# Retention's up projection by seven-product units, with mixer operands that carry the token scale

## The chip, the cores and the metric

The kernel runs on one core of one Trainium2 chip, which executes the whole program once. The metric is the device time of that execution in microseconds (us); lower is better. A kernel's time is the median of several executions.

## The reference

One decoder layer on 1024 tokens of 1024 features, in float32. Cut to what the change touches:

```python
h = rmsnorm(x, ln_mix)                 # x * rsqrt(mean(x^2)+eps) * ln_mix
z = h @ w_in                           # q | k | v | g | pu | gate_logits
ret = retention_chunkwise(rotary(q) * dk**-0.5, rotary(k), v)      # 4 heads, 8 chunks of 128
ret_n = group_norm_per_head(ret) * gn_gain
y_ret  = (silu(g) * ret_n) @ w_ret_up                              # 1024 x 1024
y_pool = (multiscale_pool(pu, windows 2/4/8/16) @ pool_w * pool_scale) @ w_pool_up
gates = sigmoid(gate_logits + b_gate)
x = x + (gates[:, :D] * y_ret + gates[:, D:] * y_pool) @ w_o
x = x + square(relu(rmsnorm(x, ln_mlp) @ w_up)) @ w_down
out = rmsnorm(x, ln_final)
```

The token scale is the `rsqrt(...)` of the first line, one number for each token.

## The kernel before

**Numbers as pairs.** Every float32 operand of a large product is carried as a pair of rounded halves, the value and its remainder (`split_pair`: one copy on ScalarE, line 134, one subtraction on VectorE, line 135). A product of two pairs is three matmuls (value by value, value by remainder, remainder by value; `PASSES`). Activations lie feature-major: 128 features on the partitions, 512 tokens (half of the sequence) in a matmul.

**Stages, in the order of TensorE's queue.** Rotary, values and retention for four heads; `pool_input(g)`, four projections to the pool channels (`ps_pu`), beside the last head; twelve *mixer units* (`ps_Xmx`, `ps_Ymx`, `ps_Zmx`, `ps_Vmx`); retention's up projection (`ps_yr`, line 630) with `pool(g)` beside it; the pool's up projection (`ps_yp`); the output projection (`ps_o`); sixteen units of the feed-forward's up projection (`ps_Xup` and so on); its down projection (`ps_dn`).

**A seven-product unit** (`seven`) computes a 256 x 1024 piece of a product as two by two blocks, by seven block products in place of eight. X, Y, Z and V are four banks of PSUM. A unit has an opening product in each bank and a closing one in X, Z and V, of 4 x 3 = 12 matmuls each, 84 in all. It needs seven stationary operands, sums of weight blocks that VectorE adds (line 192) and that are split into pairs in tag "a", and seven moving operands, each of four feature tiles, which all units of a stage share. These are combinations of the token halves of the low and high features: B11, B21 and B22 are blocks as they are, T1 to T4 are sums and differences. After a closing the function `done` finishes a quarter of the result. The first of a stage (`late`) interleaves its openings over feature tiles.

**The mixer units.** Units 0 to 3 make the swish gate g, units 4 to 11 the two branch gates. Their B operands are the tiles of `hT` (x times ln_mix, in tag "h"); `mixed_blocks` makes the T operands from another load of x in tag "r". The token scale `R1` is not in them: `done` multiplies every quarter of the result by R1 on VectorE (line 559, 566). Swish units then apply a sigmoid and multiply by the normalized retention and by gn_gain; all others apply a sigmoid, with the bias. Results go to DRAM (`ret_dram`, `sg_dram`).

**Retention's up projection** loads `ret_dram` back (`load_ret` in unit 11), splits it into 16 pairs `retT`, and makes 8 feature tiles x 2 token halves, each by 8 x 3 matmuls (384 in all), from weights loaded and split by `load_piece`. The result times the gate stays in SBUF (`m`). `pool(g)` runs after every second of these feature tiles: VectorE adds shifted copies of `u`, and six matmuls (`ps_pw`) follow for each g.

**What sets the order.** All of it is written as one program with tiles from tagged pools: tags "h" and "r" have 16 buffers of 512 KB each, "a" has 9, of which R1 holds one in the mixers; tag "raw" has two. A scheduler with a model of the engines' times then sets, before the run, each engine's own fixed sequence. On the chip every engine works through its sequence strictly in that order and waits where a tile is not ready or a buffer not free. Loads are issued by SyncE (SP), stores and some loads by GpSimd (POOL); these queues also stop at an issue that waits.

Of the kernel before, what the change touches and what calls it, by code (L numbers as in the profile page):

```python
# [30 lines left out]
NLAST = 4  # L31
EPS = 1e-6
# [6 lines left out]
def block_kernel(ctx: ExitStack, tc: tile.TileContext, a: dict, out: bass.AP):  # L39
# [12 lines left out]
    idle = apool.tile([P, HALF], mybir.dt.bfloat16, tag="a", name="idle", bufs=9)  # L52
# [123 lines left out]


    B11, B21, B22, T1, T2, T3, T4 = range(7)

    def seven(name, src, moving, done, late=False, after=None):  # L180
# [9 lines left out]
        def stationary(x, src, *adds):  # L190
            for dst, u, v in adds:
                nc.vector.tensor_tensor(dst, u, v, ALU.add)  # L192
            ws[x] = pair_tile("a", f"w{x}_{name}")
            split_pair(ws[x], src)
# [52 lines left out]
    def token_blocks(lo, hi):  # L247
        return lo[:, :HALF], lo[:, HALF:], hi[:, :HALF], hi[:, HALF:]
# [225 lines left out]

    q, k, v = [None] * NH, [None] * NH, [None] * NH
# [3 lines left out]
    for h in range(NH):  # L479
# [52 lines left out]
    ret_dram = dram_tile("ret_dram", (KT // 2, P, 2, S))  # L532
    sg_dram = dram_tile("sg_dram", (2 * KT, P, S))

    def mixer_unit(i, late=False, after=None):
# [4 lines left out]
        if swish:  # L540
            for m, f in enumerate(tiles):
                nc.gpsimd.dma_start(o[m], retn_dram[f])
        left = [2, 2]

        def done(m, half, ps, add=None):
            sl = slice(half * HALF, (half + 1) * HALF)
            dst, f = o[m][:, sl], tiles[m]
            sign = -1.0 if m else 1.0
            if swish:
                t = rpool.tile([P, 2, HALF], F32, tag="raw", name=f"sw{f}_{half}")  # L550
                z, sig = t[:, 0, :], t[:, 1, :]
# [6 lines left out]
            if swish:  # L558
                nc.vector.scalar_tensor_tensor(z, y, sign, R1[:, sl], ALU.mult, ALU.mult)
                nc.scalar.activation(sig, z, AF.Sigmoid)  # L560
                nc.vector.scalar_tensor_tensor(
                    dst, dst, vec[:, V_GNG + f : V_GNG + f + 1], sig, ALU.mult, ALU.mult
                )
                nc.vector.tensor_tensor(dst, dst, z, ALU.mult)
            else:
                nc.vector.tensor_tensor(z, y, R1[:, sl], ALU.mult)
# [9 lines left out]
    retT = []  # L576

    def load_ret():
        for p2 in range(KT // 2):
            r2 = w_tile(f"ret{p2}", F32).rearrange("p (i t) -> p i t", i=2)  # L580
            nc.sync.dma_start(r2, ret_dram[p2])
            for i in range(2):
                retT.append([])
                for half in range(2):
                    dst = pair_tile("h" if p2 < 2 else "r", f"retT{2 * p2 + i}_{half}")
                    split_pair(dst, r2[:, i, half * HALF : (half + 1) * HALF])
                    retT[-1].append(dst)

    for i in range(12):
        mixer_unit(i, late=i == 0, after=load_ret if i == 11 else None)  # L590


    pw_raw, pw = a_tile("r", "pw_raw", shape=(P, HALF)), pair_tile("r", "pw")
    nc.sync.dma_start(pw_raw, a["pool_w"])
    split_pair(pw, pw_raw)
    ypT = []

    def pool(g):
        win = WINDOWS[g]
        u = a_tile("r", f"uf{g}")  # L600
        nc.sync.dma_start(u, u_dram[g])
        cur = u
        step = 1
        while step < win:
            nx = a_tile("r", f"s{g}_{step}")
            nc.vector.tensor_copy(nx[:, :step], cur[:, :step])
            nc.vector.tensor_tensor(nx[:, step:], cur[:, step:], cur[:, : S - step], ALU.add)
            cur = nx
# [472 lines left out]
```

## Time and profile before

| | us |
|---|---|
| three runs | 1373.17, 1372.91, 1370.94 (median 1372.91) |
| the profiled execution's own time | 1370.83 |
| its span, from the first to the last instruction | 1369.0 |
| TensorE (PE) busy | 1353.6 (99%) |
| VectorE (DVE) busy | 987.9 (72%) |
| ScalarE (ACT) busy | 565.1 (41%) |
| mean granted clock of TensorE | 0.997 |

Busy times are from one profiled execution; the profile models the end of a matmul, so a busy PE says that matmuls are in flight. "PEclk" is the clock that was granted to TensorE, as a share of full speed. In a list of groups each row is a source line with its engine, operation and tiles (out<-in), then the count, the summed busy time and the mean duration, then the idle time of that engine just before these instructions and what ended it. The stages on the trace's clock: mixers from 285 to 515 us, `ps_yr` to 612, `ps_yp` to 654, up from 740 to 1060, down to the end.

### The profile page before, as it was taken

Reading aid. Unit: us, or ns where it says so; the run is one execution under the profiler, and the core shown is the slowest. Engines: PE = TensorE matmul, PEld = TensorE weight load, DVE = VectorE, ACT = ScalarE, POOL = GpSimd, SP = SyncE. Lnnn points to the kernel's source line nnn. Section 1 sums busy time; section 2 is a strip of 40 time slices with the busy share of each in tenths; the row PEclk is TensorE's granted clock in tenths of the full one; section 3 lists DMA queues with packets and bytes.
Section 4 is the critical chain, followed back from the end, with each engine's and each line's share of the span. In section 5 each row is a group of like instructions: output and inputs, shape, how many; then the busy total and the mean of one; then the engine's idle time right before and its main releaser. Section 6 shows DMA issues by size and latency. Waiting matters only on the chain. (4 is left out here: it accounts for less than half of the span.)

```text
span 1369.0 us, 17491 instructions
## 1 busy us (share of the span) xinstructions
PE 1353.6 (99%) x6572; PEld 1138.6 (83%) x6572; DVE 987.9 (72%) x1631; ACT 565.1 (41%) x960; POOL 86.1 (6%) x151
## 2 busy tenths in 40 slices
PE   9999999999999999999999999999999999999997
PEld 6998999878888888888887888888888888888886
DVE  5766565789966768628657878777787977689665
ACT  6234425463334344113445433333333544444372
POOL 0000001111000000000001011101111000000000
PEclk9999999999999999999999999999999999999999
DMA  9122021354342367124422344433437989778423
GB/s 360 50 62 77 17 92 63 124 215 158 121 172 85 112 238 261 62 77 170 154 77 77 116 169 169 151 126 147 169 139 292 407 330 351 261 266 307 159 70 123
DMA packets 65444, 225.07 MB, mean 164 GB/s; under 512 B 7376, under 2 KB 9424, under 8 KB 61264
## 3 DMA queue, kind: packets, MB, share of 16 engines
q1 hardware_dynamic: 47152, 158.66, 32.7%
q0 software_dynamic: 17920, 65.02, 12.5%
q8 instruction: 51, 0.84, 0.3%
q10 hardware_dynamic: 288, 0.29, 0.1%
q14 instruction: 33, 0.27, 0.1%
HBM read 167.31 MB, written 56.62 MB: 164 GB/s over the span
## 5 line engine op out<-in xcount | busy, mean ns | idle before, releaser
L121 PE MATMUL ps_v<-w_v_hi,hT 128*128 128x256 f32 x512 | 96.0, 284 | 0.0
L199 PE MATMUL ps_Xup<-mv,w_up 128*128 128x512 f32 x384 | 93.0, 390 | 1.7 <-DVE w_up L135 1.7
L199 PE MATMUL ps_Zup<-mv,w_up 128*128 128x512 f32 x384 | 92.5, 389 | 0.8 <-ACT w_up L134 0.8
L853 PE MATMUL ps_dnX<-db,da 128*128 128x512 f32 x384 | 93.1, 389 | 0.1
L134 ACT ACTIVATE w_up<-raw_up 128x512 fp32r<-128x512 f32 x96 | 58.3, 627 | 84.4 <-DVE raw_up L192 46.3
L199 PE MATMUL ps_Vup<-mv,w_up 128*128 128x512 f32 x384 | 92.6, 389 | 0.0
L121 PE MATMUL ps_yr<-retT,w_ret 128*128 128x512 f32 x384 | 88.5, 389 | 0.5 <-ACT w_ret L94 0.5
L121 PE MATMUL ps_o<-mixT,w_o 128*128 128x512 f32 x384 | 87.5, 389 | 0.0
L199 PEld LDWEIGHTS ps_Xup<-mv,w_up 128*128 128x128 f32 x384 | 71.9, 188 | 16.9 <-DVE w_up L135 2.1
L121 PEld LDWEIGHTS ps_yr<-retT,w_ret 128*128 128x128 f32 x384 | 72.0, 188 | 15.8 <-ACT w_ret L94 0.9
L199 PEld LDWEIGHTS ps_Zup<-mv,w_up 128*128 128x128 f32 x384 | 72.0, 188 | 15.7 <-ACT w_up L134 0.8
L853 PEld LDWEIGHTS ps_dnX<-db,da 128*128 128x128 f32 x384 | 72.0, 188 | 15.5 <-DVE db L135 0.5
L199 PEld LDWEIGHTS ps_Vup<-mv,w_up 128*128 128x128 f32 x384 | 72.0, 188 | 15.1 <-ACT w_up L134 0.2
L121 PEld LDWEIGHTS ps_o<-mixT,w_o 128*128 128x128 f32 x384 | 72.0, 188 | 15.0
L135 DVE TENSOR_TENSOR w_up<-raw_up,w_up 128x512 fp32r<-128x512 f32 x96 | 64.2, 685 | 26.4 <-ACT w_up L134 26.1
L121 PEld LDWEIGHTS ps_v<-w_v_hi,hT 128*128 128x128 f32 x512 | 80.8, 192 | 0.0
L134 ACT ACTIVATE w_mx<-raw_mx 128x512 fp32r<-128x512 f32 x72 | 43.6, 626 | 86.0 <-DVE raw_mx L192 44.0
L121 PE MATMUL ps_v<-w_v_lo,hT 128*128 128x256 f32 x256 | 72.6, 284 | 0.0
L199 PE MATMUL ps_Xmx<-hT,w_mx 128*128 128x512 f32 x288 | 72.0, 396 | 0.3 <-ACT w_mx L134 0.3
L199 PE MATMUL ps_Vmx<-hx,w_mx 128*128 128x512 f32 x288 | 69.5, 389 | 0.0
L728 ACT ACTIVATE act<-act 128x512 f32<-128x512 f32 x64 | 40.3, 629 | 65.6 <-DVE act L727 62.2
L199 PEld LDWEIGHTS ps_Xmx<-hT,w_mx 128*128 128x128 f32 x288 | 55.1, 192 | 12.5 <-ACT w_mx L134 0.6
(249 smaller groups left out, 2819.9 us busy)
## 6 DMA issues: line engine op xcount, KB each, us to landing
act_dram<-act POOLq DMA_DIRECT2D x48, 512.0 KB, 4.7
ad<-act_dram SPq DMA_DIRECT2D x48, 512.0 KB, 6.6
raw_up<-in_w_up_dram SPq DMA_DIRECT2D x16, 1024.0 KB, 5.0
raw_mx<-in_w_mix_dram SPq DMA_DIRECT2D x12, 1024.0 KB, 6.2
sg_dram<-mx POOLq DMA_DIRECT2D x16, 512.0 KB, 4.7
wa_lo<-in_w_down_dram SPq DMA_DIRECT2D x16, 512.0 KB, 9.0
wb_hi<-in_w_down_dram SPq DMA_DIRECT2D x16, 512.0 KB, 7.5
wc_lo<-in_w_down_dram SPq DMA_DIRECT2D x16, 512.0 KB, 4.3
```

The costliest lines, as they stand in the source:

```text
L121: nc.tensor.matmul(ps, stationary(k, sa), moving(k, sb), start=i == 0, stop=i == n - 1)
L134: nc.scalar.activation(dst[:, 0, :], src, AF.Copy)
L135: nc.vector.tensor_tensor(dst[:, 1, :], src, dst[:, 0, :].bitcast(F32), ALU.subtract)
L199: nc.tensor.matmul(ps, ws[x][:, sa, k * P : (k + 1) * P], moving[x][k][:, sb, :], start=start and k == 0 and n == 0, stop=k == 3 and n == ...
L728: nc.scalar.activation(dst, dst, AF.Square)
L853: nc.tensor.matmul(banks[i][:, c0 : c0 + n], w[:, sa, i * P : (i + 1) * P], x[:, sb, c0 : c0 + n], start=start and j == 0 and m == 0, stop ...
```

## The change

1. **The up projection of retention** becomes four seven-product units (`ret_unit`), 4 x 84 = 336 matmuls. The weights are laid out for it ahead of the run (`_units`). Results are multiplied by the gate, stored to `m_dram`, and loaded again beside the gate of the pool's branch in the `ps_yp` stage (`merge_parts`).
2. **All seven mixer operands** are built from x times ln_mix times R1 (one `scalar_tensor_tensor` for each of eight feature tiles), during retention (`BUILD` says after which head), as 28 pairs that go to `hx_dram` (28 x 512 KB) and are loaded into 16 "r" and 12 "h" tiles ahead of the mixers. `done` no longer multiplies by R1; gn_gain carries the sign (`gng`).
3. **Retention's moving operands** (`ret_blocks(k)`) are built the same way beside units 4, 6, 8 and 9, go to `rx_dram` and are loaded after unit 11's X bank is closed (`load_rx`).
4. **`pool(g)`** moves from the `ps_yr` stage to units 1, 3, 5 and 7 (`BESIDE`); its results go to `yp_dram` and are loaded in the last of the ret units.
5. **Buffers:** tag "a" has 5 in place of 9, a new tag "e" has 4. The mixers' stationary operands lie in "a", so five buffers (R1 is no longer held) where there were eight; the up projection of the feed-forward takes "a" and "e" in turn.

```diff
-    BUFS = {"h": 16, "r": 16, "a": 9}
+    BUFS = {"h": 16, "r": 16, "a": 5, "e": 4}
+BUILD = ((0,), (1,), (2, 3), ())
+BESIDE = {1: ("pool", 0), 3: ("pool", 1), 4: ("ret", 0), 5: ("pool", 2),
+          6: ("ret", 1), 7: ("pool", 3), 8: ("ret", 2), 9: ("ret", 3)}
+    def mixed_blocks(k):
+        blocks = []
+        for f in (k, k + 4):
+            xf = a_tile("e", f"xf{f}")
+            nc.vector.tensor_copy(xf[:, :1], R1[:, S - 1 :])
+            nc.gpsimd.dma_start(xf, a["xT"][f * P : (f + 1) * P, :])
+            nc.vector.scalar_tensor_tensor(
+                xf, xf, vec[:, V_LNM + f : V_LNM + f + 1], R1, ALU.mult, ALU.mult)
+            blocks.append(xf)
+        for x, src in moving_blocks(*blocks):      # 7 blocks, 4 of them by a sum or difference
+            t = pair_tile("e", f"hs{x}_{k}")
+            split_pair(t, src)
+            store_pair(hx_dram[4 * ORDER.index(x) + k], t)
 # mixer_unit, done():
             if swish:
-                nc.vector.scalar_tensor_tensor(z, y, sign, R1[:, sl], ALU.mult, ALU.mult)
-                nc.scalar.activation(sig, z, AF.Sigmoid)
+                nc.scalar.activation(sig, y, AF.Sigmoid, scale=sign)
                 nc.vector.scalar_tensor_tensor(
-                    dst, dst, vec[:, V_GNG + f : V_GNG + f + 1], sig, ALU.mult, ALU.mult
+                    dst, dst, gng[:, m, f : f + 1], sig, ALU.mult, ALU.mult
                 )
-                nc.vector.tensor_tensor(dst, dst, z, ALU.mult)
+                nc.vector.tensor_tensor(dst, dst, y, ALU.mult)
             else:
-                nc.vector.tensor_tensor(z, y, R1[:, sl], ALU.mult)
+    for i, x in enumerate(ORDER):                  # (B11, T2, T1, T3, B21, B22, T4)
+        for k in range(4):
+            hx[x][k] = pair_tile("rrrrhhh"[i], f"hx{x}_{k}")
+            load_pair(hx[x][k], hx_dram[4 * i + k])
+    def ret_blocks(k):                             # loads ret_dram[k], [k + 4] into tag "raw"
+        for x, src in moving_blocks(*blocks):
+            t = pair_tile("e", f"rs{x}_{k}")
+            split_pair(t, src)
+            store_pair(rx_dram[4 * ORDER.index(x) + k], t)
+    def load_rx():
+                rx[x][k] = pair_tile("errrhhh"[i], f"rx{x}_{k}")
+                load_pair(rx[x][k], rx_dram[4 * i + k])
-    for f in range(KT):
-        w = load_piece(a["w_ret"][f], f"w_ret{f}")
...
-            feature_major(ps, w, retT, half)
-            nc.vector.tensor_tensor(m[:, sl], m[:, sl], ps, ALU.mult)
+    def ret_unit(i, after=None):
+        def done(m, half, ps, add=None):
+            dst, y = o[m][:, half * HALF : (half + 1) * HALF], ps
+            if add is not None:
+                y = rpool.tile([P, HALF], F32, tag="raw", name=f"yr{tiles[m]}_{half}")
+                nc.vector.tensor_tensor(y, add, ps, ALU.add)
+            nc.vector.scalar_tensor_tensor(dst, y, -1.0 if m else 1.0, dst, ALU.mult, ALU.mult)
+            left[m] -= 1
+            if not left[m]:
+                nc.gpsimd.dma_start(m_dram[tiles[m]], o[m])
+        seven(f"ret{i}", a["w_ret"][i], rx, done, late=i == 0, after=after)
+    def merge_parts(f):                            # ps_yp stage: the gate's tile and m, from DRAM
+        nc.sync.dma_start(parts[f][:, 0, :], sg_dram[KT + f])
+        nc.sync.dma_start(parts[f][:, 1, :], m_dram[f])
```

The order of the engines' sequences changes with it. Three places follow.

TensorE where two mixer units meet. Before, units 3 and 4 (banks 3291 and 3292 are X and Y of unit 3, 3145 is Z and 3146 V of unit 2):

```order
1244 L199 MATMUL ps_Xmx_3291<-hT_0_163,w_mx_3295 128x512 x3
1245 L199 MATMUL ps_Xmx_3291<-hT_0_166,w_mx_3295 128x512 x3
1246 L199 MATMUL ps_Xmx_3291<-hT_0_169,w_mx_3295 128x512 x3
1247 L199 MATMUL ps_Xmx_3291<-hT_0_172,w_mx_3295 128x512 x3
1248 L199 MATMUL ps_Ymx_3292<-hx_0_2625,w_mx_3314 128x512 x3
1249 L199 MATMUL ps_Ymx_3292<-hx_1_2704,w_mx_3314 128x512
1250 L199 MATMUL ps_Zmx_3145<-hT_1_204,w_mx_3240 128x512 x3
```

After, units 4 and 5 (3804 and 3805 are X and Y of unit 5, 3637 is Y of unit 4; `ps_pw` belongs to `pool(1)`):

```order
1306 L213 MATMUL ps_Xmx_3804<-hx_3_2898,w_mx_3808 128x512 x3
1307 L392 MATMUL ps_pw_0_3610<-pooled_0_3607,pw_3602 128x512 x3
1308 L213 MATMUL ps_Xmx_3804<-hx_0_2924,w_mx_3843 128x512 x3
1309 L213 MATMUL ps_Xmx_3804<-hx_1_2926,w_mx_3843 128x512 x3
1310 L213 MATMUL ps_Xmx_3804<-hx_2_2928,w_mx_3843 128x512 x3
1311 L213 MATMUL ps_Xmx_3804<-hx_3_2930,w_mx_3843 128x512 x3
1312 L392 MATMUL ps_pw_1_3621<-pooled_1_3618,pw_3602 128x512
1313 L213 MATMUL ps_Ymx_3637<-hx_0_2900,w_mx_3659 128x512 x3
```

Before, a unit's Y follows its own X opening. Now the Y of unit 4 comes only behind unit 5's X opening and X closing, with its weights (3659) held in a buffer of "a" until then.

VectorE at the same place. Before, where unit 4's results are finished (`mx_0`, `mx_4`; 3704 and 3709 belong to the weights of unit 6):

```order
469 L556 TENSOR_TENSOR mx_0_3432<-tmp_mx_3436,ps_Zmx_3439 128x512
470 L192 TENSOR_TENSOR tmp_mx_3704<-raw_mx_3702 128x512
471 L566 TENSOR_TENSOR mx_0_3432<-mx_0_3432,R_130 128x512
472 L135 TENSOR_TENSOR w_mx_3709<-raw_mx_3702,w_mx_3709 128x512
473 L192 TENSOR_TENSOR raw_mx_3702<-raw_mx_3702 128x512
474 L556 TENSOR_TENSOR mx_4_3433<-tmp_mx_3436,ps_Vmx_3440 128x512
```

After (`raw_u` is the load of `pool(1)`, `win` its sums; 3743 is a weight of unit 4, 3808 to 3843 of unit 5):

```order
482 L559 COPY win_0_3594<-raw_u_3592 128x1
483 L560 TENSOR_TENSOR win_0_3594<-raw_u_3592 128x1023
484 L140 TENSOR_TENSOR w_mx_3743<-raw_mx_3633,w_mx_3743 128x512
485 L559 COPY win_1_3595<-win_0_3594 128x2
486 L560 TENSOR_TENSOR win_1_3595<-win_0_3594 128x1022
487 L140 TENSOR_TENSOR w_mx_3808<-raw_mx_3801,w_mx_3808 128x512
488 L140 TENSOR_TENSOR pw_3602<-pw_raw_3603,pw_3602 128x128
489 L563 TENSOR_TENSOR win_1_3595<-win_1_3595,corr 128x16
490 L206 TENSOR_TENSOR raw_mx_3801<-raw_mx_3801 128x512
491 L564 SCALAR_TENSOR_TENSOR win_1_3595<-win_1_3595,raw_u_3592 128x1024
492 L140 TENSOR_TENSOR w_mx_3827<-raw_mx_3801,w_mx_3827 128x512
```

The multiplications by R1 are gone, and the pool's rows stand between the weight splits, behind the load of `raw_u`.

SyncE's loads at the end of the mixers. Before:

```order
56 L182 DMA raw_mx_4372<-in_w_mix_dram 128x2048
57 L581 DMA ret_4431<-ret_dram 128x2048
58 L581 DMA ret_4445<-ret_dram 128x2048
59 L626 DMA m_4570<-sg_dram 128x1024
60 L626 DMA m_4629<-sg_dram 128x1024
```

After (`r` is the last load of `ret_blocks`, `raw_ret` the weights of a ret unit, `rx` the operands):

```order
98 L647 DMA r_4611<-ret_dram 128x1024
99 L189 DMA rx_0_4847<-rx_dram 128x1024
100 L189 DMA rx_1_4849<-rx_dram 128x1024
101 L189 DMA rx_2_4851<-rx_dram 128x1024
102 L196 DMA raw_ret_4970<-in_w_ret_dram 128x2048
103 L189 DMA rx_0_4839<-rx_dram 128x1024
```

Four loads of 1 MB and then the gates become 28 loads of operands, each into a tile that an earlier product must free, with the weights of a ret unit queued among them.

More of the change, by code (lines that the diff above doesn't have):

```diff
@@ L524, in block_kernel, with pool @@
-    pool_input(0)
-    for g in range(1, 4):
+    def pool(g):
+        win = WINDOWS[g]
+        cur = u = load_raw(u_dram[g], f"u{g}")
+        two = [a_tile("e", f"win{g}_{i}") for i in range(min(2, win // 2))]
+        step = 1
+        while step < win:
+            nx = two[(step.bit_length() - 1) % 2]
+            nc.vector.tensor_copy(nx[:, :step], cur[:, :step])
+            nc.vector.tensor_tensor(nx[:, step:], cur[:, step:], cur[:, : S - step], ALU.add)
+            cur = nx
+            step *= 2
+        nc.vector.tensor_tensor(cur[:, :16], cur[:, :16], corr[:, g, :], ALU.mult)
+        nc.vector.scalar_tensor_tensor(cur, cur, 1.0 / win, u, ALU.mult, ALU.subtract)
+        pw = consts.tile([P, 2, P], F32R, tag="mask", name=f"pw{g}")
+        pw_raw = rpool.tile([P, P], F32, tag="raw", name=f"pw_raw{g}")
+        nc.sync.dma_start(pw_raw, a["pool_w"][:, g * P : (g + 1) * P])
+        split_pair(pw, pw_raw)
+        for half in range(2):
+            pooled = pair_tile("e", f"pooled{g}_{half}")
+            split_pair(pooled, cur[:, half * HALF : (half + 1) * HALF])
+            ps = aux_bank(f"ps_pw{g}_{half}")
+            exact(ps, lambda s: pw[:, s, :], lambda s: pooled[:, s, :])
+            dst = pair_tile("e", f"yps{g}_{half}")
+            split_scaled(dst, ps, vec[:, V_PSC + g : V_PSC + g + 1])
+            store_pair(yp_dram[2 * g + half], dst)
@@ L535, in mixer_unit @@
+    for m in range(2):
+        nc.vector.tensor_scalar(
+            gng[:, m, :], vec[:, V_GNG : V_GNG + KT], -1.0 if m else 1.0, None, ALU.mult
+        )
     def mixer_unit(i, late=False, after=None):
@@ L571, in done @@
             if not left[m]:
-                nc.gpsimd.dma_start(ret_dram[f // 2, :, f % 2, :] if swish else sg_dram[f], o[m])
+                nc.gpsimd.dma_start(ret_dram[f] if swish else sg_dram[f], o[m])
         seven(f"mx{i}", a["w_mix"][i], hx, done, late=late, after=after)
[L576 to L587, printed above, removed]
@@ L589, in block_kernel @@
-    for i in range(12):
[L590 to L595, printed above, removed]
-    ypT = []
[L598 to L608, printed above, removed]
-            step *= 2
-        nc.vector.tensor_tensor(cur[:, :16], cur[:, :16], corr[:, g, :], ALU.mult)
-        nc.vector.scalar_tensor_tensor(cur, cur, 1.0 / win, u, ALU.mult, ALU.subtract)
-        ypT.append([])
-        for half in range(2):
-            pooled = pair_tile("r", f"pooled{g}_{half}")
-            split_pair(pooled, cur[:, half * HALF : (half + 1) * HALF])
-            ps = aux_bank(f"ps_pw{g}_{half}")
-            exact(ps, lambda s: pw[:, s, g * P : (g + 1) * P], lambda s: pooled[:, s, :])
-            dst = pair_tile("h", f"ypT{g}_{half}")
-            split_scaled(dst, ps, vec[:, V_PSC + g : V_PSC + g + 1])
-            ypT[g].append(dst)
@@ new lines, in block_kernel @@
+    rx = [[None] * 4 for _ in range(7)]
+    def ret_blocks(k):
+        blocks = []
+        for f in (k, k + 4):
+            r = rpool.tile([P, S], F32, tag="raw", name=f"r{f}")
+            nc.sync.dma_start(r, ret_dram[f])
+            blocks.append(r)
+        for x, src in moving_blocks(*blocks):
[3 more added lines that the diff above has]
+    def load_rx():
+        for i, x in enumerate(ORDER):
+            for k in range(4):
+                rx[x][k] = pair_tile("errrhhh"[i], f"rx{x}_{k}")
+                load_pair(rx[x][k], rx_dram[4 * i + k])
```

159 lines of the change are left out of this document (88 added, 71 removed).

## The prediction

> **What bounds the kernel now.** I read the page first: the busy shares, the slices, the chain of waits.
>
> ```profile
> span 1369.0 us, 17491 instructions
> PE 1353.6 (99%) x6572; PEld 1138.6 (83%) x6572; DVE 987.9 (72%) x1631; ACT 565.1 (41%) x960; POOL 86.1 (6%) x151
> PE 43%; DVE 1%; issue 1%; ACT 0%; POOLq 0%; POOL 0%; DVEq 0%; ACTq 0%
> ```
>
> TensorE is busy for all but 15.4 us, and nothing else has a share in the chain worth naming. So a matmul taken away is time saved, and any new wait of TensorE is time lost; work on other engines counts only when TensorE waits for it. Next, the list of TensorE's waits, for how close the others follow:
>
> ```profile
> PE ps_Xup L199 <- DVE w_up L135: 1.7, 1, 1.7
> PE ps_Zup L199 <- ACT w_up L134: 0.8, 1, 0.8
> PE ps_rt L469 <- ACT retn L472: 0.7, 1, 0.7
> PE ps_yr L121 <- ACT w_ret L94: 0.5, 1, 0.5
> PE ps_Xmx L199 <- ACT w_mx L134: 0.3, 1, 0.3
> ```
>
> Twelve mixer units give one wait of 0.3 us. The table by stretches says what cover that has (PE, PEld, DVE, ACT, POOL busy, then clock, DMA share, GB/s):
>
> ```profile
> 20.00:100.00 80.00, 80.00 (x545) 74.29 (x544) 50.19 (x82) 27.48 (x46) 2.41 (x2) 1.00 0.33 118
> 285.00:395.00 110.00, 109.93 (x477) 90.59 (x478) 95.71 (x154) 44.80 (x77) 8.51 (x16) 0.98 0.45 158
> 395.00:512.00 117.00, 117.00 (x518) 96.89 (x517) 76.16 (x119) 47.42 (x79) 6.38 (x12) 1.00 0.39 137
> 310.00:330.00 20.00, 20.00 (x90) 16.57 (x89) 19.72 (x33) 7.24 (x13) 2.13 (x4) 1.00 0.44 157
> 1040.00:1060.00 20.00, 20.00 (x89) 16.54 (x89) 14.87 (x25) 7.63 (x14) 1.24 (x3) 1.00 1.03 406
> ```
>
> At 310 to 330 VectorE is busy for 19.72 of 20 us and TensorE loses nothing: with eight buffers the weight splits run far enough ahead. The last row is the transfer engines' limit as this trace shows it, 406 GB/s, 1.3 us for 512 KB.
>
> **The gain.** The chain has the matmul's pace:
>
> ```profile
> 759.16 2.72 PE ps_Xup L199 x12
> L121 PE MATMUL ps_yr<-retT,w_ret 128*128 128x512 f32 x384 | 88.5, 389 | 0.5 <-ACT w_ret L94 0.5
> ```
>
> 12 matmuls in 2.72 us are 0.227 us each. 384 `ps_yr` matmuls become 336; 48 x 0.227 = 10.9 us go, all on the path. The 0.5 us wait goes with them, but a first weight split stands ahead of the ret units too, so I count nothing.
>
> **VectorE in the mixers.** The timeline gives its pace, the groups the counts:
>
> ```profile
> 312.40 0.68 DVE L135 TENSOR_TENSOR w_mx<-raw_mx,w_mx 128x512 fp32r<-128x512 f32 x1
> 313.00 0.69 DVE L192 TENSOR_TENSOR raw_mx<-raw_mx 128x512 f32<-128x512 f32 x1
> L566 DVE TENSOR_TENSOR mx<-mx,R 128x512 f32<-128x512 f32 x24 | 16.5, 687 | 0.3
> L559 DVE SCALAR_TENSOR_TENSOR sw<-sw,R 128x512 f32<-128x512 f32 x12 | 8.2, 684 | 0.1
> L561 DVE SCALAR_TENSOR_TENSOR mx<-mx,vec,sw 128x512 f32<-128x512 f32 x16 | 11.9, 743 | 0.0
> L611 DVE SCALAR_TENSOR_TENSOR s<-s,uf 128x1024 f32<-128x1024 f32 x4 | 4.9, 1224 | 0.1
> ```
>
> One 128x512 row takes 0.60 us from start to start (312.40 to 313.00), 0.66 where it has a scalar for each partition. A sigmoid unit has 7 weight splits, 4 weight sums, 2 for u2 and u4, 3 sums of results and 4 multiplications by R1: 20 rows, 12.0 us. Without R1 it is 16, 9.6 us. A swish unit falls from 28 rows, 17.0 us, to 24, 14.6. Added is `ret_blocks`, 4 sums and 7 splits, 6.6 us each, and `pool(g)`: sums of 1.2 us (the 128x1024 row), four splits and small copies, 5.5 us for g = 0 and 1.4 more for each further window, so 5.5 to 9.7. By pairs of units: 0 and 1 with pool 0, 34.7 us; 2 and 3, 36.1; 4 and 5 with ret 0 and pool 2, 34; 6 and 7, 35.5; 8 and 9, 32.4; 10 and 11, 19.2. (The scheduler lets each pool slip into the next pair; the sum stays.) TensorE needs 2 x 84 x 0.227 = 38.1 us for a pair, 39.4 with six `ps_pw`, which were there before. So VectorE stays under TensorE in every pair, at 82 to 92%; load alone costs nothing, and the cover of 310 to 330 was thinner.
>
> What is new is the order with five buffers in place of eight. The Y weights of the even unit are held until the odd unit's X is closed, so four buffers turn over, and each split waits for a product to end before the row can run, with the pool's rows of 1.2 us queued between. A late split holds TensorE: the one such row of this trace is the 1.7 us at `ps_Xup`. I take 1.0 us for each of the four pool places (between 0, as at 310 to 330, and 1.7), 4.0 in sum, 0 to 6.8.
>
> At units 4 and 5 there is one thing more. The load of `raw_u` needs a buffer of tag "raw" (two, shared with the sigmoid's scratch of unit 3), and the pool's first copy waits for it; behind that copy stand a V weight of unit 4 and the X weight of unit 5.
>
> ```profile
> uf<-u_dram SPq DMA_DIRECT2D x4, 512.0 KB, 4.9
> raw_mx<-in_w_mix_dram SPq DMA_DIRECT2D x12, 1024.0 KB, 6.2
> ret_dram<-mx POOLq DMA_DIRECT2D x8, 512.0 KB, 5.1
> ```
>
> If the buffer comes free just before, the whole 4.9 us is waited for by VectorE; TensorE has the products split already, some 2.7 us of them. I take 2.0 (0 to 4.9).
>
> **The mixers' operands.** 28 x 512 KB are 36 us of the transfer engines at 1.3 us each, where before nothing was loaded but weights. The place:
>
> ```profile
> 264.54 16.62 PE L121 MATMUL ps_pu<-hT,w_pu 128*128 128x512 f32 x72 [0.22 <-DVE u L504]
> 281.00 1.91 PE L469 MATMUL ps_rt<-ident,rn 128*128 128x128 f32 x11
> 283.08 0.33 PE L469 MATMUL ps_rt<-ident,rn 128*128 128x128 f32 x1 [0.17 <-ACT rn L456]
> 284.07 0.66 PE L469 MATMUL ps_rt<-ident,rn 128*128 128x128 f32 x4 [0.67 <-ACT retn L472]
> 285.07 4.87 PE L199 MATMUL ps_Xmx<-hT,w_mx 128*128 128x512 f32 x12 [0.34 <-ACT w_mx L134]
> 276.00:285.00 9.00, 7.79 (x39) 5.77 (x37) 8.27 (x16) 9.00 (x18) 2.72 (x5) 1.00 0.94 335
> 285.00:289.00 4.00, 3.93 (x10) 2.85 (x11) 2.59 (x4) 3.52 (x8) 1.06 (x2) 0.61 0.98 398
> ```
>
> In the new order 67 `ps_pu` matmuls (15.2 us) and the 16 transposes (4.1 us with their waits, as here) lie between the last product that frees an "r" tile and X. Some eight of the 16 "r" loads are done by then, the other eight need 10.5 us, the next weights 2.6: all are in 6 us before X. The twelve "h" loads follow as the last pool input frees tile after tile, 15.7 us, to 10 us after X; the first is needed at unit 0's X closing, 48 matmuls or 10.9 us after X. It fits by about a microsecond, with stores of `retn`, `u` and the next weights in the same queues. I take 1.0 (0 to 6: a queue that is as full as at 276 to 289, at 335 GB/s, takes 18% longer on 36 us).
>
> **Retention's operands.** Again 28 loads. Four lie in "e" and wait for the last stores of `ret_blocks(3)` on POOL's queue, behind which the gates' stores stand; the T tiles come free only through unit 11's openings, the last "h" tiles at its end. From about 19 us before the first ret product, 16 loads end about 2 us after it, and that unit's openings use them over 10.9 us. SP's queue holds the ret weights behind the first three. I take 2.0 (0 to 6, as above).
>
> **Small terms.** VectorE gets 8 scalings (1.3 us) and 44 rows of 0.6 early, 37 us, and loses 16 sums and 16 splits before the mixers; its idle 30 us of 80 at 20 to 100 covers that, and in-order splits of qT and kT slip behind a few of these rows: 0.5 (0 to 2). 28 stores to `hx_dram` share POOL's queue with `retn`: nothing, since these are read much later. The `ps_yp` stage loads 1 MB for each of 8 tiles in 44 us, some 190 GB/s: nothing (0 to 2). The feed-forward's ring is seven buffers as before: nothing (1 either way, its first split is that 1.7 us). Without R1 nothing shrinks on TensorE.
>
> **Sum.** -10.9 + 4.0 + 2.0 + 1.0 + 2.0 + 0.5 = -1.4 us. The profiled execution took 1370.83 us (1369.0 of span and 1.8 around it), so 1369.4 for one like it. It stands 2.1 below the median of the runs, 1372.91; against that I predict 1371.5. All low ends together give 1372.91 - 11.9 = 1361; all high ends -10.9 + 30 = +19, or 1392.
>
> **The clock.** At 285 to 289 the granted clock was 0.61: after transposes and 1.2 us of waits, 12 matmuls took 4.87 us in place of 2.72, which is 2.15 us lost. At 740 to 749 there are longer waits and the clock stays full:
>
> ```profile
> 743.06 2.55 PE L199 MATMUL ps_Xup<-mv,w_up 128*128 128x512 f32 x10 [1.67 <-DVE w_up L135]
> 747.15 0.73 PE L199 MATMUL ps_Zup<-mv,w_up 128*128 128x512 f32 x2 [0.75 <-ACT w_up L134]
> 736.00:750.00 14.00, 11.49 (x57) 8.91 (x56) 11.45 (x22) 8.40 (x15) 3.57 (x4) 1.00 0.35 142
> ```
>
> So my waits of 1 to 2 us cost themselves only; if each of the seven brought 2.15 us more, the sum would be +13.7. [...]
>
> **Rivals.**
> - *The cover holds everywhere* (0.28). For it: TensorE lost nothing at 310 to 330 beside a full VectorE. Against it: that was with eight buffers. The mixers' 6.0 go to about 1, the loads stay: -10.9 + 1 + 3.5 = -6.4, 1366.5.
> - *Five buffers pace every unit* (0.16), slower. A split then waits in every unit for a buffer that the product before it frees, not only beside a pool. At 1.7 us (the row at `ps_Xup`) in eight of the twelve units that is 13.6 in place of 4.0: -10.9 + 13.6 + 2.0 + 3.5 = +8.2, 1381.1. Since 13.65 us of losses (10.9 + 2.75) make the kernel measurably slower and the other terms hold 5.5, it decides from 8.2 us, or 0.7 us in each unit. Against it: VectorE is full in no pair.
> - *The operands come late* (0.11), slower. Both blocks at 6 us, the half-speed spell once more at 2.15: -10.9 + 6 + 12 + 0.5 + 2.15 = +9.8, 1382.7. For it: 335 GB/s at 276 to 285, and three queues; against it: the openings of a late unit take the tiles one by one.
> - My forecast, *most of the gain is given back* (0.45): 1371.5, within 1367 to 1376.
>
> **Chances.** A measurement of this kernel tells 0.2%, 2.75 us, from no change: faster is below 1370.2, slower above 1375.7. Of the forecast's 0.45 I put 0.16 below, 0.27 within, 0.02 above. So faster 0.16 + 0.28 = 0.44, same 0.27, slower 0.29. The range from 1363 to 1383 leaves out some 0.03 below and 0.1 above.
>
> **What would show it.** `ps_Xret` and its kin with 336 matmuls in about 76 us; waits of TensorE in the mixers at the X openings and closings of the odd units, released by a weight split; VectorE waiting for `raw_u` near unit 4's end; the DMA share near 1 for 30 us around 270 and 510; the clock at 1.00 away from the mixers' start. I am wrong if waits of `hx` or `rx` loads lead the list, or if `ps_Xmx` waits in units without a pool.

## The result, and the profile after

The changed kernel takes 1386.32 us (1385.64 to 1386.7), the kernel before 1372.91: 1.0103 of it, 95% interval 1.0086 to 1.012. It is 13.4 us slower, above the range of the prediction. (Single executions of a kernel can take far longer than its others, one of before 1499.21 us and one with half the bytes 4812.86; the ratios here leave these out.) The page of the profiled execution, then TensorE's list of waits (engine, line, releaser: us in total, times, longest):

```profile
span 1384.5 us, 17942 instructions
PE 1352.5 (98%) x6524; PEld 1128.5 (82%) x6524; DVE 1021.0 (74%) x1700; ACT 581.6 (42%) x1003; POOL 135.3 (10%) x251
PE 56%; DMA 6%; issue 3%; DVE 3%; ACT 1%; POOL 1%; SPq 0%; POOLq 0%; DVEq 0%; ACTq 0%
```

```profile
PE ps_Xmx L213 <- ACT w_mx L139: 2.8, 4, 0.8
PE ps_Zret L213 <- DMA rx<-rx_dram: 2.8, 3, 1.0
PE ps_Zmx L213 <- DMA hx<-hx_dram: 2.5, 2, 1.5
PE ps_Xmx L213 <- DVE w_mx L140: 2.0, 2, 1.2
PE ps_Zret L213 <- ACT w_ret L139: 1.6, 1, 1.6
...
PE ps_Vret L213 <- DVE yr L680: 1.0, 1, 1.0
PE ps_pw L392 <- DVE pooled L140: 1.0, 2, 0.8
```

Transfers have entered the chain (6%, before none), and the waits of mixers and ret units have grown from 0.8 us to some 17. No wait is longer than 1.63 us, and the list alone doesn't add up to the loss. The starts of the stages on the two timelines do, with the 24 `ps_pw` matmuls (5.4 us), which moved between stages, taken out, and with the 11 matmuls of the first ret unit that run ahead of the last mixer product counted with the ret units:

| from, to | before | after | difference |
|---|---|---|---|
| start to the first `ps_Xmx` | 285.1 | 283.6 | -1.5 |
| to the end of the mixers | 230.5 | 242.8 | +12.3 |
| `ps_yr` or ret units, with `ps_yp`, to the first `ps_o` | 131.3 | 134.6 | +3.3 |
| to the last transposes of the token scale (`spread_z`) | 709.8 | 708.5 | -1.3 |

So two stages lose: the mixers 12.3 us, and the ret units 14.2, since they have 10.9 us less to do. (Of the 15.5 us between the two spans 2.6 lie behind the last VectorE instruction, where both kernels do the same; that tail was 3.9 to 6.5 us in the profiles here. I did not follow it. Before, `ps_yr` ends at 608 and `ps_yp` at 652 us, 1.5 to 4.5 us earlier than the stage list ahead of the prediction has them.)

**The ret units.** The timeline of TensorE at their start (start, duration, then in brackets the idle time ahead and what ended it), SyncE's issues, what these waited for (500 to 560 us), the table by stretches, and at last the two queues' traffic from 535 to 548 us (q1 is SyncE's, q0 GpSimd's: packets, MB, share of the engines):

```profile
535.41 0.96 PE L213 MATMUL ps_Yret<-rx,w_ret 128*128 128x512 f32 x3
538.00 0.94 PE L213 MATMUL ps_Zret<-rx,w_ret 128*128 128x512 f32 x3 [1.63 <-ACT w_ret L139]
539.96 1.65 PE L213 MATMUL ps_Zret<-rx,w_ret 128*128 128x512 f32 x3 [1.03 <-DMA rx<-rx_dram]
542.51 1.65 PE L213 MATMUL ps_Xret<-rx,w_ret 128*128 128x512 f32 x3 [0.90 <-DMA rx<-rx_dram]
545.08 1.65 PE L213 MATMUL ps_Zret<-rx,w_ret 128*128 128x512 f32 x3 [0.93 <-DMA rx<-rx_dram]
547.54 1.65 PE L213 MATMUL ps_Zret<-rx,w_ret 128*128 128x512 f32 x3 [0.81 <-DMA rx<-rx_dram]
549.40 4.08 PE L213 MATMUL ps_Vret<-rx,w_ret 128*128 128x512 f32 x9 [0.22 <-DMA rx<-rx_dram]
```

```profile
508.25 1.68 SPq L189 DMA_DIRECT2D rx<-rx_dram  x3
...
511.03 9.10 SPq L189 DMA_DIRECT2D rx<-rx_dram  x3
...
520.75 32.75 SPq L189 DMA_DIRECT2D rx<-rx_dram  x20
```

```profile
SPq L189 <- DMA rx<-rx_dram: 26.2, 20, 2.3
SPq L189 <- PE ps_Xmx L213: 21.8, 6, 13.5
```

```profile
500.00:530.00 30.00, 30.00 (x134) 24.86 (x133) 22.92 (x36) 15.05 (x25) 5.60 (x13) 1.00 1.01 392
536.00:555.00 19.00, 13.22 (x32) 7.45 (x31) 3.33 (x6) 2.13 (x5) 1.08 (x2) 0.64 1.03 413
```

```profile
q1 hardware_dynamic: 761, 2.77, 52.7%
q0 software_dynamic: 704, 2.62, 49.9%
```

Three matmuls, 0.68 us of work, alternate with a wait, the first time for a weight split, then for the next operand. From 539.96 on the three last 1.65 in place of 0.96 us: the mean granted clock is 0.64 from 536 to 555. Twenty of the 28 loads are issued only between 520.8 and 553.5, one behind the other, while the transfer engines are full (share 1.01 and 1.03) and VectorE is idle for 16 of 19 us. Start to start these rows take 13.8 us more than their matmuls at 0.227 us (with 1.2 and 0.8 us at 581 and 588). Some 7 us of that are the waits in brackets: 4 of them for `rx`, the others for late weight splits (1.6 and 0.6) and for a result row on VectorE (1.0). Some 4.6 are the clock (0.69 in each of the four rows of 1.65, 1.9 in the nine V matmuls), and the other 2 lie around the waits, where the matmuls take longer (the last section has a case).

Two things made the operands late, one after the other. SyncE's first six loads, up to 519.8, waited for tiles, five of them for an X product of the last mixer units; at the fifth the queue stood for 7 us (512.0 to 519.1). From 523.0 to 562.4 each issue comes within 0.1 us of the landing of the load eight places earlier: the tiles were free, and the transfers set the pace. No issue of SyncE precedes the landing of the one eight places before it in this trace. With the engines to themselves the loads land every 1.28 us (549 to 560, 409 GB/s), but from 535.4 to 547.5 every 2.0 to 2.6 us, since GpSimd's queue, which stores and reloads gates, takes half. So by 531.1, 2 us after the first ret product (529.13), only six of the 28 had landed.

**The mixers.** In the same table:

```profile
310.00:400.00 90.00, 86.26 (x369) 68.02 (x368) 78.34 (x126) 38.55 (x67) 9.47 (x21) 1.00 0.47 171
400.00:500.00 100.00, 97.56 (x426) 79.22 (x425) 84.52 (x140) 52.18 (x90) 19.44 (x44) 1.00 0.73 268
```

and on the timeline at the first pool:

```profile
338.97 3.31 PE L213 MATMUL ps_Xmx<-hx,w_mx 128*128 128x512 f32 x12 [0.65 <-ACT w_mx L139]
342.12 0.39 PE L392 MATMUL ps_pw<-pooled,pw 128*128 128x512 f32 x1
343.30 0.73 PE L392 MATMUL ps_pw<-pooled,pw 128*128 128x512 f32 x2 [0.79 <-DVE pooled L140]
```

The waits cost more than their brackets: the 12 matmuls behind the 0.65 us take 3.15 us to the next start (338.97 to 342.12) in place of 2.72. So counted from start to start, the four pool places lose some 3.7, 2.1, 1.3 and 2.6 us and the late `hx` loads with the first products 3.6.

### The profile page after: what moved, and what is told of

Read it like the earlier page. It is cut to its first block, busy times and chain, and to the rows that moved or that the text cites. A ratio compares the mean times of both kernels' runs of the same rounds, so it can differ in the third digit from the quotient of the medians.

```text
span 1384.5 us, 17942 instructions
## 1 busy us (share of the span) xinstructions
PE 1352.5 (98%) x6524; PEld 1128.5 (82%) x6524; DVE 1021.0 (74%) x1700; ACT 581.6 (42%) x1003; POOL 135.3 (10%) x251
## 4 chain that ended last, share of the span: by engine, by line
PE 56%; DMA 6%; issue 3%; DVE 3%; ACT 1%; POOL 1%; SPq 0%; POOLq 0%; DVEq 0%; ACTq 0%
PE ps_o L126 6%; PE ps_dnZ L912 6%; PE ps_dnX L912 6%; PE ps_dnV L912 6%; PE ps_Xup L213 6%; PE ps_Zup L213 5%; PE ps_Vup L213 5%; PE ps_yp L126 3%; DMA rx<-rx_dram 3%; PE ps_Yup L213 3%; PE ps_dnY L912 3%; PE ps_Vret L213 1%; PE ps_Xret L213 1%; PE ps_Zret L213 1%; DMA rx_dram<-rs 1%
## 5 line engine op out<-in xcount | busy, mean ns | idle before, releaser
L213 PE MATMUL ps_Xmx<-hx,w_mx 128*128 128x512 f32 x288 | 72.4, 395 | 4.7 <-ACT w_mx L139 2.8
L213 PE MATMUL ps_Zmx<-hx,w_mx 128*128 128x512 f32 x288 | 71.3, 391 | 3.4 <-DMA hx<-hx_dram 2.5
L213 PEld LDWEIGHTS ps_Xmx<-hx,w_mx 128*128 128x128 f32 x288 | 53.0, 188 | 20.4 <-DVE w_mx L140 5.3
L140 DVE TENSOR_TENSOR w_mx<-raw_mx,w_mx 128x512 fp32r<-128x512 f32 x72 | 49.0, 689 | 24.7 <-ACT w_mx L139 24.5
## 6 DMA issues: line engine op xcount, KB each, us to landing
act_dram<-act POOLq DMA_DIRECT2D x48, 512.0 KB, 5.4
ad<-act_dram SPq DMA_DIRECT2D x48, 512.0 KB, 6.2
hx_dram<-hs POOLq DMA_DIRECT2D x28, 512.0 KB, 3.6
hx<-hx_dram SPq DMA_DIRECT2D x28, 512.0 KB, 12.2
rx_dram<-rs POOLq DMA_DIRECT2D x28, 512.0 KB, 4.6
rx<-rx_dram SPq DMA_DIRECT2D x28, 512.0 KB, 12.0
```

The source lines that it names most:

```text
L140: nc.vector.tensor_tensor(dst[:, 1, :], src, dst[:, 0, :].bitcast(F32), ALU.subtract)
L213: nc.tensor.matmul(ps, ws[x][:, sa, k * P : (k + 1) * P], moving[x][k][:, sb, :], start=start and k == 0 and n == 0, stop=k == 3 and n == ...
```

## The experiments

My theories: the mixers lose to the pool's rows in the queue of the weight splits (1), and the ret units to the bytes of their operand loads (2). Rivals: five buffers pace every unit; the loads wait for tiles to come free or for their place in SyncE's queue; the ret units wait for their own weight splits. Kernels of before, run beside each group, had medians of 1371.1 to 1371.8.

**Nothing beside the mixers (e1).**

```diff
     for i in range(12):
-        mixer_unit(i, late=i == 0, after=load_rx if i == 11 else None)
-        if i in BESIDE:
...
+        mixer_unit(i, late=i == 0)
+    for n in range(4): ret_blocks(n)
+    for n in range(4): pool(n)
+    load_rx()
```

> The pool and the four blocks of retention's operands run after the twelve mixer units and not beside them; the rest is as in the changed kernel. Only the stretch of the mixers is to be read (in the changed kernel 248 us from the first ps_Xmx to the last ps_Vmx, 243 without the 24 ps_pw, of which 228.5 are matmuls at 0.227 us). Theory 1, the pool's rows between the weight splits hold TensorE: the stretch falls to 231 to 233 us, and only the 2.5 us for late hx loads remain. Rival, five buffers pace every unit: it stays at 238 us or more, with waits at X openings. The whole time rises by the VectorE work that now lies open, to 1420 to 1445 us.

1425.0 us. The stretches of the mixers:

```profile
310.00:400.00 90.00, 89.49 (x393) 73.21 (x393) 78.58 (x125) 38.89 (x67) 12.22 (x27) 1.00 0.57 195
400.00:500.00 100.00, 100.00 (x443) 82.81 (x442) 77.61 (x123) 50.67 (x86) 17.10 (x41) 1.00 0.68 248
```

TensorE is idle for 0.5 us in 190, with the same ring of five: the rival falls. From 310 to 400 VectorE is as busy as in the changed kernel (78.58 and 78.34 us of 90), so its load alone isn't what costs there. The late `hx` loads cost more here (some 6 us up to 308), so the whole stretch is some 237 us, above what I gave. Whether a pool would cost less with eight buffers no run here tests.

**The old up projection of retention in the changed kernel (e3).** (`load_ret`, `load_piece` and 384 matmuls in place of `ret_blocks`, `load_rx` and `ret_unit`; mixers and pool as changed.)

> Retention's up projection is done by 8 x 2 x 24 matmuls as before; its operands come by four loads and 16 splits, none through DRAM as pairs. Mixers, pool beside units 1, 3, 5, 7 and hx through DRAM stay. Theory 1, late rx loads and the half clock behind them cost 14 us in the ret units: from the end of the mixers to the first ps_o 131 to 133 us (134.65 in the changed kernel, with 10.9 us less of matmuls), no half clock near 540, whole time 1380 to 1384. Rival, the loss comes from VectorE and the weight splits, which also stand here: 140 us or more there and 1390 or more in all.

1379.24 us (1377.53 to 1382.01), 7.1 less than the changed kernel in spite of 48 more matmuls. From the end of the mixers to the first `ps_o` nothing is lost but one wait of 1.2 us, and the clock stays at 1.00 there: theory 2 holds as to the place, but this run takes away the stores, the splits and the loads together. The mixers here show where a pool costs:

```profile
310.00:400.00 90.00, 86.79 (x371) 68.42 (x370) 78.08 (x127) 36.80 (x64) 8.94 (x20) 1.00 0.46 160
400.00:500.00 100.00, 100.00 (x443) 82.81 (x442) 68.92 (x109) 43.55 (x71) 9.67 (x28) 1.00 0.49 176
```

The two pools near swish units lose as before, the two beside sigmoid units nothing, once the blocks of retention's operands are gone.

**Half the bytes (e6).** The product is then not retention's any more; only the time is of use.

```diff
-                        ps, ws[x][:, sa, k * P : (k + 1) * P], moving[x][k][:, sb, :],
+                        ps, ws[x][:, sa, k * P : (k + 1) * P], moving[x][k][:, 0 if moving is rx_ref else sb, :],
...
-                rx[x][k] = pair_tile("errrhhh"[i], f"rx{x}_{k}")
-                load_pair(rx[x][k], rx_dram[4 * i + k])
+                rx[x][k] = a_tile("errrhhh"[i], f"rx{x}_{k}", F32R, (P, 1, HALF))
+                nc.sync.dma_start(rx[x][k].bitcast(F32), rx_dram[4 * i + k][:, :1, :])
```

> The ret units' 28 operand loads move half the bytes: only the first half of each pair (7.3 MB in place of 14.7) is loaded and stands in all three matmuls; the remainder of retention's operands is left out of the result. Nothing else changes. Theory 2, the transfer engines' bandwidth makes the rx loads late (DMA share 1.0 from 500 to 555): waits on rx and the half clock near 540 go, some 10 to 13 us less, 1373 to 1377. Rival, each load waits for its tile to be freed or for its place in SP's queue: the waits stay, 1383 to 1387.

1371.7 us, 14.6 below the changed kernel (ratio to before 1.0002, 0.9992 to 1.0011), a little below what I gave. The bytes are not all that changed: the scheduler's sequences differ within the ret units. The second load of ret weights (1 MB) stands behind 23 operand loads where it stood behind six, which alone brings the operands forward by 2.6 us (an estimate, 1 MB at 406 GB/s), and the order of the first ret products differs. So the run agrees with theory 2, but by itself it doesn't exclude the place in the queue. That the bytes set the pace from 523 us on is shown by the landings in the changed kernel's own trace, above; there the rival of the tiles holds for the first loads, up to 519.8, and that of the weight splits for 2.2 us of the waits.

**Other covers and places that did not help.** The first half of `ps_yp` ahead of the ret units, as cover (e4; its theory 1 is what is the rival of the tiles above):

> The first token half of ps_yp (96 matmuls, 21.8 us) runs between the last mixer unit and the first ret unit; its products with the gate go to DRAM and are added later. It needs four weight pieces loaded and split twice. Theory 1, rx loads are late because they can only start when unit 11 frees its tiles: 21.8 us of cover takes the waits on rx and the half clock away, 10 to 14 us less, 1372 to 1377. Rival, the ret units wait for their weight splits: the waits stay at 8 us or more and the time at 1384 or above.

1406.14 us. The cover waits for a load itself:

```profile
539.63 6.42 PE L126 MATMUL ps_yp<-ypT,w_po 128*128 128x512 f32 x15 [4.12 <-DMA ypT<-yp_dram]
549.16 5.18 PE L126 MATMUL ps_yp<-ypT,w_po 128*128 128x512 f32 x15 [3.12 <-DMA ypT<-yp_dram]
```

Its operands come through the same full engines as those it was to hide (DMA share 1.03 from 520 to 540); as a test of theory 2 it tells nothing. Blocks earlier, pool later, by the table alone (e5; `BESIDE`: ret 3 to 6, pool 7 to 10):

> Only the table is changed: blocks of retention's operands beside units 3 to 6, the pool beside units 7 to 10. Theory 1a, a pool costs where VectorE is full: beside units with 9.6 us of VectorE work it costs under 1 us each, the mixers lose 4 to 6 us and not 14; the stores to rx_dram end some 40 us earlier, so the transfer engines have less to do at 500 to 530 and the rx waits halve: 1370 to 1376. Rival 1b, the pool's chain (long rows in the same queue as the splits, with a ring of five) costs 3 us wherever it stands, and rx loads wait for tiles, not for bandwidth: 1383 to 1387.

1391.18 us. The transfer engines were still full to 560, and one wait for a load was longer than any before (the waits' row, then the stretch):

```profile
PE ps_Xret L213 <- DMA rx<-rx_dram: 11.2, 3, 9.8
```

```profile
545.00:560.00 15.00, 4.68 (x19) 2.91 (x17) 2.05 (x3) 1.26 (x2) 1.07 (x2) 0.82 1.03 414
```

So 1a failed, and the time is above 1b's too. The first three pools cost 1.1 to 1.4 us each, start to start, not under 1; the last waited 4.3 us for its operands, and behind it twelve matmuls took 5.08 us in place of 2.72, at a granted clock of 0.79 in the mean from 515 to 530. Only the blocks earlier (e9; ret 4, 5, 6, 7):

> Only the table is changed: the blocks of retention's operands beside units 4, 5, 6, 7 (in the changed kernel 4, 6, 8, 9); the pool stays at 1, 3, 5, 7. Theory 2, the 14.7 MB of stores to rx_dram share the transfer engines with the loads at 500 to 515: with the stores earlier the ret units lose 5 to 9 us in place of 14, and the mixers lose 12 to 14 as before: 1377 to 1382. Rival, the loads alone fill the engines whenever they come: within 2 us of 1386.

1388.74 us. Here the waits on `rx` are gone but for 0.3 us, and the ret units lose 5.6 us, as I expected. The earlier stores helped the loads: the fourteenth landed 31 us after the first issue, in the changed kernel 39. But the ret units also begin 8.4 us later, which hides some of the loads too (v3a, below, has the earlier stores without that). The last pool, pushed to where blocks and pool meet, waits 5.3 us for its operands, and weight splits follow late: some 15 us are lost from 460 to 492. What is won at one place is lost at the other.

**The pool in the retention stage.** Whole (v3a; each behind its projection, without `u_dram`):

> Each pool runs right behind its projection in the retention stage, from SBUF without u_dram, where VectorE is busy for 14 of 35 us (250 to 285); the blocks of retention's operands stand beside units 4 to 7. Theory 1, the pool's rows between the weight splits cost the mixers 6 to 8 us: they go, 4 to 6 us stay for hx and ret blocks. Theory 2, with the stores to rx_dram over 40 us before unit 11's end the rx waits fall from 14 to 5 to 10. Together 1368 to 1377. Rival: the pools delay the last head's chain or the first weight splits of the mixers, so the mixers start 5 us later or more, 1378 to 1390.

1412.86 us: the mixers lose about 1 us in all, with retention's blocks beside them, but the pools run one behind the other ahead of them, with nothing for TensorE beside (ahead of the brackets, start and duration):

```profile
286.83 2.07 PE L125 MATMUL ps_pu<-hT,w_pu 128*128 128x512 f32 x4 [13.86 <-ACT w_pu L98]
310.87 1.95 PE L391 MATMUL ps_pw<-pooled,pw 128*128 128x512 f32 x3 [9.01 <-ACT pooled L138]
```

Its ret units, which begin at 563, don't wait for `rx` at all, though all 28 loads still move full pairs; they lose some 9 us to a late weight split (2.3), a late result row (2.7) and what follows these. The stores are over early, and the engines have room ahead of 563:

```profile
520.00:540.00 20.00, 20.00 (x90) 16.58 (x89) 10.90 (x16) 8.39 (x14) 1.26 (x4) 1.00 0.14 55
540.00:563.00 23.00, 23.00 (x103) 19.07 (x102) 11.12 (x17) 7.68 (x14) 1.06 (x2) 1.00 0.74 275
```

So theory 2 is to be put more widely: not the loads' bytes alone, but these together with the stores, weights and gates of the same stretch make the loads late.

The first ret unit in plain order, on top of this (v3b):

> As v3a, and the first ret unit runs its products in the usual order, one bank after the other, not interleaved over feature tiles, so that each opening needs only four operands, in the order in which the loads come. Theory 2, operands arrive at 0.76 tiles a us and the interleaved openings ask for 16 at once: 2 to 5 us less than v3a. Rival, all 28 are needed within 19 us either way: the same within 1 us.

1418.13 us, 5 more than v3a and not less: one wait of 6.9 us for `rx` (8.4 us of them in all), where v3a has none. With only the window sums in the retention stage, and the pool's splits and products at units 1, 2, 3, 5 (v7):

> The pool's window sums (14 long VectorE rows) run in the retention stage right behind the projections and go to u_dram in u's place; only the splits and products of a pool stand beside the mixers (units 1, 2, 3, 5), retention's blocks beside 4 to 7. Theory 1, it is the long rows and the load in the splits' queue that hold TensorE: the pool places cost under 1 us each, the mixers lose 6 us (hx 4 of them); with the earlier stores 1370 to 1376. Rival, the even unit's Y held behind the odd unit's X is what costs at a pool place, and that stays: mixers lose 11 to 14, 1377 to 1382.

1382.69 us. The mixers still lose some 10 us from 329 to 397, as the rival had it: short rows in a full queue cost as well. It is the place more than the rows' length. What holds TensorE at such a place, the full VectorE or the Y that waits for the next unit's X, this run doesn't separate.

**Operands unsplit through DRAM (v10c).** The loads carry float32 sums, and the split comes after:

```diff
     def ret_blocks(k):
...
+        for n, t in enumerate(ts):          # T1 to T4, float32
+            for i in range(2):
+                nc.gpsimd.dma_start(t_dram[2 * n + i, k], t[:, i, :])
     def load_rx():
...
+                nc.sync.dma_start(t[:, 1, :].bitcast(F32), src)   # ret_dram or t_dram
+                nc.scalar.activation(t[:, 0, :], t[:, 1, :].bitcast(F32), AF.Copy)
+                nc.vector.tensor_tensor(t[:, 1, :], t[:, 1, :].bitcast(F32),
+                                        t[:, 0, :].bitcast(F32), ALU.subtract)
```

> Retention's operands go through DRAM unsplit: the sums T1 to T4 are stored in float32 (4 MB in place of 14.7), the blocks B are read from ret_dram, 28 loads of 256 KB (7.3 MB) land in the second half of each pair's tile, and the 28 splits run after the load, on ScalarE and VectorE, which have slack there (24 of 45 us busy at 500 to 545 in v7). All else is as in the changed kernel, the table of places too. Theory 2, it is the bytes: as with half the bytes before (1371.7), 10 to 15 us less, 1371 to 1377. Rival, the 28 splits (17 us of VectorE) take the loads' place as what the first ret unit waits for: 1380 or more.

1369.31 us (1367.29 to 1371.43): 0.9983 of before, 0.9972 to 0.9995, and 17.0 us below the changed kernel. At the ret units' start (500 to 530, 530 to 560) and in the mixers:

```profile
500.00:530.00 30.00, 29.75 (x130) 24.07 (x130) 18.94 (x30) 15.82 (x28) 1.06 (x2) 1.00 0.67 235
530.00:560.00 30.00, 28.45 (x124) 22.91 (x124) 26.27 (x44) 16.46 (x30) 4.28 (x8) 1.00 0.79 309
310.00:400.00 90.00, 85.86 (x367) 67.78 (x366) 78.77 (x127) 36.57 (x63) 11.12 (x24) 1.00 0.51 178
400.00:500.00 100.00, 100.00 (x443) 82.88 (x442) 79.69 (x130) 45.65 (x76) 16.21 (x40) 1.00 0.62 222
```

The clock stays full, the waits at 500 to 560 are 1.8 us; the splits find room on VectorE. Taken from beside the mixers, they also free the two pools there (400 to 500), as in e3. So the 17.0 us are the gain at both places together. With the window sums in the retention stage and the pool at units 7 to 10 (v10):

> As v10c, and the pool's window sums run in the retention stage as in v7; its products stand beside units 7 to 10 and retention's sums beside units 4 to 7. Theory 1, a pool of short rows beside a sigmoid unit (9.6 us of VectorE in 19) costs nothing, and without the 28 splits beside the mixers still less: the mixers lose 4 to 6 us (hx) and not 14: 1362 to 1370, faster than before. Rival, the pool's long rows in the retention stage delay the mixers' first splits, or the late stores of yp keep the transfer engines full at unit 11: 1372 or more.

1376.71 us. At 400 to 500 TensorE lost nothing, but a wait of 5.1 us for `tmp_ret`, a ScalarE copy, came at the ret units, where pool and 28 splits meet. Then v10c with all pools beside sigmoid units, two tables (v11b: pool 5, 7, 8, 9 with ret 4, 6, 7, 9; v11c: pool 4, 6, 8, 10 with ret 5, 7, 9, 9):

> v10c with another table only: the four pools beside the sigmoid units 5, 7, 8 and 9 and retention's sums beside 4, 6, 7 and 9, none beside the swish units 1 and 3. Theory 1, a pool costs TensorE time where VectorE is full (swish units: 14.6 + 5.5 to 6.9 us in 19, with a ring of five) and nothing beside sigmoid units (9.6 us): the 5.9 us lost at 325 to 385 in v10c go, 1362 to 1366. Rival, the pool's rows in the splits' queue cost some 2 us wherever they stand: 1368 to 1371.

> As v11b with the pools beside units 4, 6, 8 and 10, one in every second unit, and retention's sums beside 5, 7 and 9. Theory 1: as v11b, 1362 to 1366, if the last pool at unit 10 does not delay the ret units' first splits; its rows stand beside the 28 splits of the loaded operands, and then 1366 to 1372. Rival, 2 us a pool wherever it stands: 1368 to 1372.

v11b 1368.9 us (0.9979 of before, 0.997 to 0.9989), v11c 1376.25. Stretches of v11b, then a wait of v11c:

```profile
310.00:400.00 90.00, 89.49 (x393) 73.28 (x392) 76.43 (x122) 36.34 (x62) 10.20 (x24) 1.00 0.53 182
400.00:500.00 100.00, 100.00 (x441) 82.48 (x441) 77.81 (x126) 45.45 (x77) 14.37 (x35) 1.00 0.54 192
```

```profile
PE ps_Xret L218 <- ACT rx L673: 4.2, 1, 4.2
```

In v11b the some 6 us that v10c lost at 325 to 385 are gone: theory 1 holds as to the place. But the time, 1362 to 1366 by theory 1, is the rival's: it falls by only 0.4 us, less than the two intervals tell apart. From 520 to 533, behind the pool at unit 9, 4 to 5 us of new losses stand, and in the profiled execution the clock fell to half for 3.4 us at 301.6 (0.93 in the mean from 285 to 310). In v11c the pool at unit 10 delays the splits by 4.2 us and more. v11b has the lowest median found, 2.7 us below before (v10c, 2.4 below, can't be told from it); it realizes a quarter of the 10.9.

## Why the prediction was wrong, point by point

- **The gain**, 48 x 0.227 = 10.9 us: right, the ret units have 336 matmuls and, where operands are there, take 0.227 us each.
- **Retention's operands**: the step that failed most. I took 2.0 (0 to 6); the ret units lose 13.8, of which 3.2 us of waits are for weight splits and a result row and not for these loads. The loads were costed as if they had 406 GB/s to themselves from 19 us ahead, so that 16 would have landed 2 us after the first ret product. Six had. These were issued by 520, behind tiles that the last mixer units freed late, and stores, weights and gates shared engines that were already full at 500 to 530 (share 1.01). Twenty more came at 320 GB/s (20 x 0.524 MB in 32.75 us), the last two from 558 on. With half the bytes and a changed order the kernel took 14.6 us less.
- **The clock**: the sentence that waits of 1 to 2 us "cost themselves only" failed in the ret units. Six waits of 0.2 to 1.6 us in a row, with 0.7 us of work between, went with a granted clock of 0.64 from 536 to 555, some 4.6 of the 13.8 us there. My third rival had the half clock once, at 2.15 us.
- **The pool in the mixers**: 4.0 + 2.0 taken, 9.7 measured. The mechanism was right (late weight splits behind the pool's rows, `raw_u` ended a VectorE wait of 0.95 us at 377), the size not: I priced one wait for each place, by its bracket; there are one to four, each with up to 0.6 us more than its bracket. e3 and v11b put the cost at the swish units, but what makes these places dear, beside VectorE's load, is argued and not shown.
- **Load alone**: that 82 to 92% costs nothing by itself held where nothing stood between the weight splits (e1, VectorE at 87% from 310 to 400, 0.5 us idle) and at sigmoid units without the 28 splits (v10c, 80% from 400 to 500, nothing). At the same 87% with two pools among them the changed kernel was idle for 3.7 us there. So the load did not tell where TensorE would wait.
- **The mixers' operands**: 1.0 taken, 3.6 measured; but the half-clock spell of before at 285 was gone (1.00 from 283 to 290), and X started 1.5 us earlier, since the splits of the operands that `mixed_blocks` made there no longer stand ahead of it. On balance nothing, and the 0.5 for the retention stage was a gain.
- **The rivals**: the result is the third (operands late) with the pool's cost on top, at 1386 and not 1382.7. "Five buffers pace every unit" is refuted by e1, for units with nothing beside them. Of the signs that I named, `hx` and `rx` waits near the top of the list are there.
- **Sums**: the high ends add up to 28.7 and not 30, so to 1390.7; 335 in place of 406 GB/s makes a load 21% longer, not 18%; and 30 us of idle VectorE at 20 to 100 do not by themselves cover 37 us of rows. None of these changes the forecast.

## What to carry to other kernels

When a change sends operands through DRAM, sum all bytes of the stretch, stores and weights too, against the full rate that the trace shows (here 413 GB/s from 536 to 555) from the moment at which the first buffer comes free: the time saved on TensorE, 10.9 us, was smaller than that of these transfers, 36 us for the 28 loads alone (an estimate, 14.7 MB at 406 GB/s). Send the unsplit form if the engines that split have room where the loads land: with it this kernel took 17.0 us less. Side work belongs beside units in which VectorE has slack of its own; a pool cost 2 to 4 us near the swish units and nothing beside the sigmoid units of e3 (VectorE busy for 68.92 us of 100 there), where no other side work stood.

## What was unexpected of the hardware

The clock fell without any long wait: none ahead of 539.96 was over 1.63 us.

```profile
536.00:539.60 3.60, 1.31 (x5) 0.49 (x3) 2.46 (x4) 0.69 (x2) 0.96 (x2) 1.00 1.03 415
539.60:553.20 13.60, 10.39 (x21) 5.99 (x22) 0.69 (x1) 0.63 (x1) 0.12 (x1) 0.50 1.03 413
```

In the 3.6 us ahead of the fall TensorE was busy for 1.31, in two pieces, and then the granted clock was 0.50 for 13.6 us, four times 3.4; in v11b, from 301.6 (0.93 in the mean from 285 to 310), and in the kernel before, from 285.9, it was 0.50 for 3.4 us. A like pattern at 297 to 302 of the changed kernel (waits of 1.48 and 0.98 us) left the clock at 1.00, and in v11b, with waits of 0.27, 1.44 and 0.90 us, did not. What tells the two apart, and what sets the length of a spell, no trace here shows. The longest single wait, by which the prediction went, does not: 1.48 us left the clock at full, 1.44 did not.

One matmul group behind a wait was slower at the granted full clock (1.00 from 338.9 to 342.2): 3.15 us from start to start for 12, in place of 2.72, at 338.97.
